# Neighbourhood attention with two heads' keys and queries in one tile, scores by 64 rows, a third set of bias tables

## The chip, the cores and the metric

The kernel runs on one core of one Trainium2 chip. The core has the matrix engine PE (weights are loaded into it by LDWEIGHTS, listed apart as PEld, and the other operand streams past), the vector engine DVE, the scalar engine ACT, the engine POOL, and a queue SP from which almost all DMAs of this kernel are issued. Each engine carries out its own list of instructions in order; engines wait for each other on semaphores. The metric is the device time of one execution in microseconds, as the median of several runs.

## What is computed

One layer of a hybrid backbone over 1024 latent and 256 context tokens of width 1024: an input projection, a gated delta rule scan in two directions over four heads (group A), 2-D neighbourhood attention over eight heads of 64 (group B), an output projection and a SwiGLU feed-forward. The change concerns group B. Cut to what matters:

```python
def neighborhood_attention(q, k, v, k_ctx, v_ctx, rpb, rows):
    ...
        q_r = lax.dynamic_index_in_dim(qg, r, axis=1, keepdims=False)
        k_r = lax.dynamic_slice_in_dim(kg, r0, win_rows, axis=1)[:, :, key_cols]
        v_r = lax.dynamic_slice_in_dim(vg, r0, win_rows, axis=1)[:, :, key_cols]
        ...
        s_win = jnp.einsum("bnqhd,binchd->bhnqic", q_r, k_r) + bias
        s_win = jnp.where(col_valid[:, :, None, :], s_win, -jnp.inf)
        s_ctx = jnp.einsum("bnqhd,bkhd->bhnqk", q_r, k_ctx)
        s = jnp.concatenate([s_win.reshape(B, H, N_COL_BLK, QB_W, n_win), s_ctx], axis=-1)
        p = jax.nn.softmax(s, axis=-1)
        o = (jnp.einsum("bhnqic,binchd->bnqhd", p_win, v_r)
             + jnp.einsum("bhnqk,bkhd->bnqhd", p[..., n_win:], v_ctx))
```

Each latent query has one softmax over its window (with a learned bias) and all 256 context keys.

## The kernel before

**Stages.** Up to about 540 us the kernel computes the projections (class `Block`, tiles blk, hh, hl, whi, wlo), and beside them the inverses of 32 x 32 blocks (N, WK, ut) and the preparation of the scan's chunks (`preps`: kk, fx, y, matmuls pr). Then the scan (`scan`, two directions, ten chunks each; its matmuls have ps as output) and neighbourhood attention (`attention`) run interleaved up to about 765 us. The output projection and the feed-forward follow.

**Attention by pairs of heads.** `attention` is a generator. It walks over 32 units: four pairs of heads, and for each 8 blocks of 128 queries (TILES). A unit is one call of `pair`, which has three parts, separated by yields: the scores of both heads and their softmax (tile sc in PSUM, then ex), the transposes of the probabilities (again sc, copied by ACT to pt), and the product with the values (vc for context, vw for the window), whose result goes to na. The first part of unit n+1 is issued before the second part of unit n. Scores, transposes and values share three PSUM slots of 1024 float32 each (`slot`).

**Scores.** Queries and keys have 64 dimensions and are kept as two float16 numbers, a high and a low part, whose sum is the float32 value. Before, the 128 rows of the array hold for one head the high part of the queries in the first 64 and the low part in the last 64 (qs), and the keys' high part stands twice, in both halves (kh), and so does the low part (kl). One matmul with kh and one with kl so give all four products of high and low. A head has 640 scores a query, 256 context and 384 window ones, in a PSUM slot that starts at column 0 for the first head and 128 for the second (AT, WIN, CTX), so that no matmul crosses a bank.

**Values.** The two heads of a unit write to two halves of the columns of the array (64 columns each), in turn.

**Softmax.** DVE adds the bias table and takes the maximum (L364), negates it (L365), ACT takes the exponential with its sum (L366), DVE inverts the sum (L367) and scales (L368). The bias tables bt (two, one for each head) exist in two sets; `biases` loads the next set by DMA (L325).

**What sets the order.** `beside` draws the attention forward by PACE = 0.72 steps for each step of a scan direction. The order on each engine is then made by a scheduler from the program's order and its estimate of when things are ready, so an edit at one place can move instructions elsewhere. Some matmuls are pinned in program order; those of attention are not.

**Storage.** The normed keys and queries are written to DRAM by `Block.norm` (L574, tile hl16, one DMA for each part and head) and loaded by `load` in `attention` (L306 to L309, five DMAs a head). A float32 matmul shows in the trace as two instructions, a float16 one or a transpose as one.

## Time and profile before

| | |
|---|---|
| runs | 1516.56, 1509.77, 1509.48 us; median 1509.77 |
| profiled execution | 1511.45 us, its span 1509.7 us |
| granted clock of PE, mean | 0.99 |
| HBM traffic | 201.01 MB read, 68.98 MB written |
| scores, kh and kl together | 320 matmuls, 74.3 us busy |
| transposes of ex | 320 matmuls, 45.9 us busy |
| values, vc and vw together | 640 instructions, 83.2 us busy |

A row of the timeline gives start, duration, engine, line, operation, output<-inputs, for a matmul rows*columns of the array that it uses, the shape and type of its operand, and how many instructions are merged (x8). PE is pipelined: a matmul's duration holds the way through the array, so several stand in the trace at once, and their pace is read from the starts. Busy time of PE therefore overstates how much it does. In brackets stands for how long the engine sat idle before, and what ended that.

### The profile page before, as it was taken

The page shows a single profiled execution, that of the slowest core. Times are in us where ns is not written, and L with a number is a line of the kernel's source. Part 1 is how long each engine was busy: PE and PEld are TensorE (multiplying, and loading weights), DVE is VectorE, ACT ScalarE, POOL GpSimd, SP SyncE. Part 2 cuts the span into 40 slices and gives each one's busy share as a digit, 9 for nine tenths or more (in the row PEclk, how much of TensorE's full clock was granted, in tenths as well). Part 3 has the DMA queues.
Part 4 walks back from the last instruction along what each step waited for, and adds up shares of the span by engine and source line. Part 5 has one row for each costly group of instructions (what it writes and reads, how often), then busy time and mean ns, then how long its engine had stood idle before and what let it go on. Part 6 is the DMA issues. An engine that isn't in the chain of part 4 may idle for free.

```text
span 1509.7 us, 23086 instructions
## 1 busy us (share of the span) xinstructions
PE 1453.5 (96%) x8365; PEld 1205.7 (80%) x8365; DVE 1007.9 (67%) x1908; ACT 704.7 (47%) x1379; POOL 164.6 (11%) x191
## 2 busy tenths in 40 slices
PE   6999998799999999999989999999999999999998
PEld 2789887678877778898777888788888888888887
DVE  4886579445587418789966499655555666698652
ACT  6443362585256536667732374333333334354441
POOL 0153500243134300000000000000000000000000
PEclk9999999999999999999999999999999999999999
DMA  9377133566378799986339216333333325798742
GB/s 366 119 237 234 35 107 121 180 180 194 98 235 249 214 272 289 264 225 184 116 119 313 99 35 208 106 105 105 105 105 105 104 94 173 267 365 281 237 153 84
DMA packets 198851, 267.35 MB, mean 177 GB/s; under 512 B 15232, under 2 KB 106960, under 8 KB 197712
## 3 DMA queue, kind: packets, MB, share of 16 engines
q1 hardware_dynamic: 198016, 265.49, 55.1%
q8 instruction: 66, 1.08, 0.3%
q10 hardware_dynamic: 720, 0.37, 0.1%
q14 instruction: 49, 0.40, 0.1%
HBM read 201.01 MB, written 68.98 MB: 179 GB/s over the span
## 4 chain that ended last, share of the span: by engine, by line
PE 67%; DVE 8%; DMA 5%; ACT 5%; issue 2%; SPq 1%; POOL 0%; ACTq 0%; DVEq 0%; POOLq 0%
PE ps L102 45%; PE blk L102 10%; PE sc L102 5%; PE pr L102 3%; DMA nv_d<-zt 2%; PE sc L106 2%; PE m L102 1%; DMA wad<-wa 1%; DMA wraw<-w_nqk 1%; DVE acc L256 1%; ACT ex L366 1%; DVE x L1616 1%; DVE cacc L520 1%; SPq L1093 1%; DVE ex L368 0%
## 5 line engine op out<-in xcount | busy, mean ns | idle before, releaser
L102 PE MATMUL ps<-hT,uhi 128*128 128x512 f32 x496 | 146.8, 390 | 0.9 <-DVE e L1737 0.8
L102 PE MATMUL ps<-lT,uhi 128*128 128x512 f32 x496 | 146.4, 389 | 0.0
L102 PE MATMUL ps<-hT,ulo 128*128 128x512 f32 x496 | 146.2, 389 | 0.0
L102 PE MATMUL blk<-hh,whi 128*128 128x512 f32 (+1 forms) x456 | 139.3, 397 | 2.1 <-ACT hh L748 1.8
L102 PE MATMUL blk<-hl,whi 128*128 128x512 f32 (+1 forms) x456 | 130.1, 379 | 0.0
L102 PE MATMUL blk<-hh,wlo 128*128 128x512 f32 (+1 forms) x456 | 129.9, 378 | 0.0
L102 PE MATMUL ps<-hB,uhi 128*128 128x512 f32 x436 | 129.1, 390 | 0.0
L102 PE MATMUL ps<-lB,uhi 128*128 128x512 f32 x436 | 128.9, 389 | 0.0
L102 PE MATMUL ps<-hB,ulo 128*128 128x512 f32 x436 | 128.7, 389 | 0.0
L1446 ACT CAST uhi<-ws 128x512 fp32r<-128x512 f32 x91 | 54.7, 623 | 145.4 <-PE ps L102 75.8
L1446 ACT CAST uhi<-wq 128x512 fp32r<-128x512 f32 x101 | 60.4, 621 | 130.8 <-PE ps L102 66.3
L1447 DVE TENSOR_TENSOR ulo<-wq,uhi 128x512 fp32r<-128x512 f32 x101 | 67.1, 686 | 65.6 <-ACT uhi L1446 36.1
L102 PEld LDWEIGHTS ps<-hT,uhi 128*128 128x128 f32 x496 | 92.9, 188 | 20.7 <-ACT uhi L1446 1.2
L102 PEld LDWEIGHTS ps<-lT,uhi 128*128 128x128 f32 x496 | 93.0, 188 | 19.7 <-DVE lT L1600 0.4
L102 PEld LDWEIGHTS ps<-hT,ulo 128*128 128x128 f32 x496 | 93.1, 188 | 19.4
L102 PEld LDWEIGHTS ps<-hB,uhi 128*128 128x128 f32 x436 | 81.8, 188 | 17.4 <-issue 0.5
L102 PEld LDWEIGHTS ps<-lB,uhi 128*128 128x128 f32 x436 | 81.8, 188 | 17.3 <-DVE lB L1600 0.4
L102 PEld LDWEIGHTS ps<-hB,ulo 128*128 128x128 f32 x436 | 81.8, 188 | 17.0
L102 PEld LDWEIGHTS blk<-hh,wlo 128*128 128x128 f32 x456 | 80.9, 191 | 17.9 <-issue 1.7
L102 PEld LDWEIGHTS blk<-hl,whi 128*128 128x128 f32 x456 | 81.6, 192 | 15.5
L102 PEld LDWEIGHTS blk<-hh,whi 128*128 128x128 f32 x456 | 77.3, 192 | 19.4 <-ACT hh L748 3.7
L1447 DVE TENSOR_TENSOR ulo<-ws,uhi 128x512 fp32r<-128x512 f32 x91 | 60.6, 685 | 36.2 <-ACT uhi L1446 28.1
(337 smaller groups left out, 3020.1 us busy)
## 6 DMA issues: line engine op xcount, KB each, us to landing
wq<-w_fo SPq DMA_DIRECT2D x99, 256.0 KB
wq<-w_gu SPq DMA_DIRECT2D x88, 256.0 KB
wad<-wa SPq DMA_DIRECT2D x64, 256.0 KB
t_d<-g SPq DMA_DIRECT2D x22, 512.0 KB
fr<-t_d SPq DMA_DIRECT2D x44, 256.0 KB
bt<-rpb SPq DMA_DIRECT2D x48, 192.0 KB
f_d<-g SPq DMA_DIRECT2D x33, 256.0 KB
fr<-f_d SPq DMA_DIRECT2D x33, 256.0 KB
```

Source lines behind the costliest of these rows:

```text
L102: i = nc.tensor.matmul(*args, **kw)
L106: i = nc.tensor.transpose(*args, **kw)
L256: dve.scalar_tensor_tensor(acc2, x, sc, acc2, op0=OP.mult, op1=OP.add)
L366: act.activation(ex, ex, AF.Exp, bias=m[:, 1:2], accum_out=m[:, 2:3])
L520: dve.scalar_tensor_tensor(acc[:, d0:d1], raw[:, d0 + o:d1 + o], cw[:, blk, tap:tap + 1], acc[:, d0:d1], op0=OP.mult, op1=OP.add)
L1093: sp.dma_start(vw_d[:, cb, ch], vlat[4 * ch:4 * ch + 4, BLKS[cb]:BLKS[cb] + 32])
L1446: act.copy(hi, self.raw[key])
L1447: dve.tensor_tensor(lo, self.raw[key], hi.bitcast(F32), OP.subtract)
L1616: dve.tensor_tensor(B[at][:, k], B[x][:, k], B.get(y, B["B11"])[:, k], OP.subtract)
```

## The change

Keys and queries of two heads share a tile: the 64 dimensions of the first head in the first 64 rows, of the second in the last 64; high and low parts lie behind one another. A unit's scores become 24 matmuls of 64 rows: three parts (256 context, 256 and 128 window scores), for each the four products of high and low, for each the two heads in turn on the two row halves, into two PSUM slots. Context comes first for both heads, so AT, WIN and CTX go, and the order of the values is the same for both. Keys and queries are stored by one DMA a block instead of four and loaded by two a pair of heads instead of ten. The room this frees holds a third set of bias tables, a fifth ex and a fourth pt.

```diff
-    nq_d = dram.tile([NAH, 2, ND, L], F16, name="nq_d", tag="nq_d")
-    nk_d = dram.tile([2, NAH, ND, T], F16, name="nk_d", tag="nk_d")
+    nq_d = dram.tile([NAH // 2, 128, 2, L], F16, name="nq_d", tag="nq_d")
+    nk_d = dram.tile([NAH // 2, 128, 2, T], F16, name="nk_d", tag="nk_d")
...
-        def load(hd):
-            qs = nw.tile([128, L], F16, name="qs", tag="qs", bufs=4)
-            kh = nw.tile([128, T], F16, name="kh", tag="kh", bufs=4)
-            kl = nw.tile([128, T], F16, name="kl", tag="kl", bufs=4)
-            sp.dma_start(qs, nq_d[hd].rearrange("i d t -> (i d) t"))
-            for i in range(2):
-                sp.dma_start(kh[i * 64:i * 64 + 64], nk_d[0, hd])
-                sp.dma_start(kl[i * 64:i * 64 + 64], nk_d[1, hd])
-            return qs, kh, kl
+        def queries(hp):
+            qs = nw.tile([128, 2, L], F16, name="qs", tag="qs", bufs=2)
+            sp.dma_start(qs, nq_d[hp])
+            return qs
+
+        def keys(hp):
+            kx = nw.tile([128, 2, T], F16, name="kx", tag="kx", bufs=2)
+            sp.dma_start(kx, nk_d[hp])
+            return kx
...
-                      for i in range(2)]
+                      for i in range(3)]
...
-                out = lasting_bt[tables[1] % 2]
+                out = lasting_bt[tables[1] % 3]
...
-            for u, (head, w0, bt) in enumerate(zip(heads, WIN, bts)):
-                qs, kh, kl = head
-                sc = slot()[:, AT[u]:AT[u] + 640]
-                q = qs[:, (half * 4 + cb) * 128:(half * 4 + cb + 1) * 128]
...
-                for n0, n1, ks in parts:
-                    for i in range(2):
-                        pe.matmul(sc[:, n0:n1], q, ks[i], start=i == 0, stop=i == 1)
+            qs, kx = heads
+            scs = [slot()[:, :640] for _ in range(2)]
+            q = [[qs[u * ND:u * ND + ND, i, (half * 4 + cb) * 128:(half * 4 + cb + 1) * 128] for i in range(2)]
+                 for u in range(2)]
+            kw = [[kx[u * ND:u * ND + ND, i, CT:].rearrange("p (r c) -> p r c", c=64)[
+                :, r0:r0 + 12, BLKS[cb]:BLKS[cb] + 32] for i in range(2)] for u in range(2)]
+            for n0, n1, part in ((0, CT, None), (CT, 512, slice(0, 8)), (512, 640, slice(8, 12))):
+                for j in range(4):
+                    for u in range(2):
+                        k = kw[u][j % 2][:, part] if part else kx[u * ND:u * ND + ND, j % 2, 0:CT]
+                        pe.matmul(scs[u][:, n0:n1], q[u][j // 2], k, start=j == 0, stop=j == 3)
+            for u, (sc, bt) in enumerate(zip(scs, bts)):
                 m = mx[:, u]
-                ex = nw.tile([128, 640], F32, name="ex", tag="ex", bufs=4)
+                ex = nw.tile([128, 640], F32, name="ex", tag="ex", bufs=5)
...
-                pt = nw.tile([128, 640], F32, name="pt", tag="pt", bufs=3)
+                pt = nw.tile([128, 640], F32, name="pt", tag="pt", bufs=4)
...
-                for i, x in enumerate((h16, l16)):
-                    for hb in range(2):
-                        hd = 2 * self.i + hb
-                        dst = nk_d[i, hd] if isk else nq_d[hd, i]
-                        sp.dma_start(dst, x[hb * 64:hb * 64 + 64, t0:])
+                sp.dma_start((nk_d if isk else nq_d)[i], hl16[:, :, t0:])
```

The scheduler makes a new order from this, in two places that matter below.

The first is on PE late in the attention, between the scores of one unit (sc<-kh,qs and sc<-kl,qs), the values of the unit before (sc<-pt,vc and sc<-pt,vw) and the transposes that follow (sc<-cst,ex). Before:

```order
L102 LDWEIGHTS qs
L102 MATMUL sc<-kh,qs 128x384
L102 LDWEIGHTS qs
L102 MATMUL sc<-kl,qs 128x384
L102 MATMUL sc<-pt,vc 64x128
L102 MATMUL sc<-pt,vw 64x128
L102 MATMUL sc<-pt,vc 64x128
L102 MATMUL sc<-pt,vw 64x128 x4
L102 MATMUL sc<-pt,vc 64x128
L102 MATMUL sc<-pt,vw 64x128
L102 MATMUL sc<-pt,vc 64x128
L106 MATMUL sc<-cst,ex 128x128 x10
```

And now, with the tiles' numbers (sc_6953 is the first head's slot, sc_6954 the second's, sc_6882 the slot of the unit before):

```order
L99 MATMUL sc_6953<-kx_6389,qs_6184 128x256
L99 LDWEIGHTS qs_6184
L99 MATMUL sc_6954<-kx_6389,qs_6184 128x256
L99 LDWEIGHTS qs_6184
L99 MATMUL sc_6954<-kx_6389,qs_6184 128x256
L99 LDWEIGHTS qs_6184
L99 MATMUL sc_6953<-kx_6389,qs_6184 128x256
L99 LDWEIGHTS qs_6184
L99 MATMUL sc_6954<-kx_6389,qs_6184 128x256
L99 LDWEIGHTS qs_6184
L99 MATMUL sc_6953<-kx_6389,qs_6184 128x256
L99 MATMUL sc_6882<-pt_6880,vc_6186 64x128
```

The values now cut into a unit's scores after 7 of 24, and the other 17 follow them; before, a unit's ten scores stood whole ahead of them here.

The second place is on DVE in the projection stage, where the block inverses end (ut and WK are their transposed and scaled forms, which go to DRAM as x_d for the scan's preparation) beside the norm of the last block of keys (cacc, hl). Before:

```order
L967 STREAM_TRANSPOSE ut<-WK 128x1280
L970 TENSOR_TENSOR ut<-ut,NB 128x1280
L556 SCALAR_TENSOR_TENSOR cacc<-cacc,qkw,cr 128x1280
L967 STREAM_TRANSPOSE ut<-WK 128x1280
L562 TENSOR_TENSOR hl_2523<-cacc,hl_2523 128x1280
L970 TENSOR_TENSOR WK<-WK,NB 128x1280
L556 SCALAR_TENSOR_TENSOR cacc<-cacc,qkw,cr 128x1024
```

Now:

```order
L958 STREAM_TRANSPOSE ut<-WK 128x1280
L961 TENSOR_TENSOR ut<-ut,NB 128x1280
L958 STREAM_TRANSPOSE ut<-WK 128x1280
L551 SCALAR_TENSOR_TENSOR cacc<-cacc,qkw,cr 128x1280
L961 TENSOR_TENSOR WK<-WK,NB 128x1280
L557 TENSOR_TENSOR hl_2514<-cacc,hl_2514 128x1280
L1007 TENSOR_TENSOR kk<-kk,e 128x512 x2
```

The second transpose moved ahead of cacc, and hl behind the scaling of WK. On PE, the first matmul of the preparation (pr<-fx,kk) stands 16 matmuls of the projection earlier than before.

More of the change, by code (lines that the diff above doesn't have):

```diff
@@ L53 @@
 NCONST = 4 * 128 + 4 * 32
-WIN = (256, 0)
-AT = (0, 128)
 TILES = ((0, 0), (0, 1), (1, 1), (2, 1), (2, 0), (1, 0), (3, 0), (3, 1))
-CTX = {256: slice(0, 256), 0: slice(384, 640)}
 PACE = 0.72
@@ L322, in biases @@
             if tables[0] != key:
-                out = lasting_bt[tables[1] % 2]
-                for u, w0 in enumerate(WIN):
-                    sp.dma_start(out[u][:, w0:w0 + 384], a["rpb"][2 * hp + u, half, CASE[cb]])
+                out = lasting_bt[tables[1] % 3]
+                for u in range(2):
+                    sp.dma_start(out[u][:, CT:], a["rpb"][2 * hp + u, half, CASE[cb]])
                 tables[:] = key, tables[1] + 1
-            return lasting_bt[(tables[1] - 1) % 2]
+            return lasting_bt[(tables[1] - 1) % 3]
         def values(hp, half, cb):
@@ L380, in pair @@
             yield 1
-            o = held[:, AT[1] + 640:AT[1] + 768]
+            o = held[:, 640:768]
+            vals = [vc[:, i] for i in range(2)] + [vw[:, i] for i in range(3)]
             for j in range(5):
-                for u, (w0, pt) in enumerate(zip(WIN, pts)):
-                    vals = [vc[:, i] for i in range(2)] + [vw[:, i] for i in range(3)]
-                    vv = (vals[j] if w0 else vals[(j + 2) % 5])[:, u * ND:u * ND + ND]
+                for u, pt in enumerate(pts):
+                    vv = vals[j][:, u * ND:u * ND + ND]
                     pe.matmul(o[u * ND:u * ND + ND], vv, pt[:, j * 128:(j + 1) * 128], start=j == 0, stop=j == 4)
@@ L394, in attention @@
         order = [(hp, half, cb) for hp in range(NAH // 2) for cb, half in TILES]
-        heads = {0: [load(0), load(1)]}
+        heads = {0: [queries(0), keys(0)]}
         vcs = {0: context(0)}
@@ L402, in attention @@
             if at in (4, 6) and hp + 1 < NAH // 2:
-                heads.setdefault(hp + 1, []).append(load(2 * hp + at // 2))
+                heads.setdefault(hp + 1, []).append((queries if at == 4 else keys)(hp + 1))
                 if at == 4:
```

14 lines of the change are left out of this document (4 added, 10 removed).

## The prediction

> **What bounds the kernel now.** I read the page first, then the busy time of the stretches in which neighbourhood attention runs, then what PE waits for there, and last single instructions. The page's engine line says PE; the scores run only between 555 and 765 us, so two stretches of that time matter.
>
> ```profile
> PE 1453.5 (96%) x8365; PEld 1205.7 (80%) x8365; DVE 1007.9 (67%) x1908; ACT 704.7 (47%) x1379; POOL 164.6 (11%) x191
> ```
>
> ```profile
> core 0: us, PE busy (x) PEld busy (x) DVE busy (x) ACT busy (x) POOL busy (x), PEclk, DMA share, GB/s
> 555.00:672.00 117.00, 113.98 (x1106) 101.75 (x1103) 92.58 (x306) 79.35 (x214) 0.00 (x0) 1.00 0.96 262
> 672.00:765.00 93.00, 88.00 (x860) 75.36 (x858) 86.96 (x345) 65.26 (x179) 2.57 (x2) 1.00 0.50 150
> ```
>
> ```profile
> 671.06 1.06 PE L102 MATMUL ps<-vn,y 128*128 128x128 f32 x8
> ```
>
> The row of PE's timeline marks the boundary: the vn,y matmuls of the seventh scan step. Up to there PE is busy 97% and DVE 79%: PE alone is the limit, and what is added to PE is added to the time. Behind it the output gates of the scan are on DVE as well: DVE is busy 93.5%, PE 94.6%. There PE has 5 us in which it stands still, and added work hides in part behind DVE. DMA is full in the first stretch (0.96), so the question is whether anybody waits for a landing. The waits of PE, of its weight loads (PEld) and of the SP queue answer it:
>
> ```profile
> PE sc L102 <- ACT pt L378: 2.0, 4, 1.0
> PE sc L106 <- DVE ex L368: 2.0, 1, 2.0
> PE sc L106 <- DVE mx L364: 1.1, 3, 0.5
> PEld sc L102 <- ACT pt L378: 7.3, 18, 1.4
> SPq L325 <- DVE mx L364: 22.2, 13, 7.4
> ```
>
> PE's longest totals are 2.0 us, all for ACT or DVE and none for a DMA. SP's queue does stand 22.2 us behind a bias table that is still in use (L325), which is what the third set takes away; but no engine's list of waits shows a landed table, key or query being late. So I cost the fewer loads (40 issues of keys and queries before, 8 now) and the third table at nothing: the prefetch already covers them. If that cover were gone, the price would be at most those 22.2 us of queue, in a stretch with DMA half idle.
>
> **The scores themselves.** A pair of heads has 10 score matmuls of 128 rows before, 2 x 2 x 640 columns, and 24 of 64 rows now, 2 x 4 x 640 columns. What a column costs, and what it costs PE to change the shape in which its array is used, stands in one place of the trace, where the value matmuls (128*64: two halves of the columns, vc and vw are tiles of values) come between whole-array matmuls:
>
> ```profile
> 594.37 1.06 PE L102 MATMUL ps<-vn,at 128*128 128x128 f32 x8
> 595.36 0.32 PE L102 MATMUL sc<-pt,vc 128*64 128x128 f32 x1
> 595.36 0.32 PE L102 MATMUL sc<-pt,vw 128*64 128x128 f32 x1
> 595.52 0.27 PE L102 MATMUL sc<-pt,vc 128*64 128x128 f32 x1
> 595.52 0.27 PE L102 MATMUL sc<-pt,vw 128*64 128x128 f32 x1
> 595.62 0.27 PE L102 MATMUL sc<-pt,vc 128*64 128x128 f32 x1
> 595.63 0.27 PE L102 MATMUL sc<-pt,vw 128*64 128x128 f32 x1
> ...
> 596.18 0.27 PE L102 MATMUL sc<-pt,vc 128*64 128x128 f32 x1
> 596.38 1.16 PE L102 MATMUL ps<-vk,kt 128*128 128x128 f32 x8
> 597.47 0.32 PE L102 MATMUL sc<-pt,vw 128*64 128x128 f32 x1
> ...
> 597.63 0.27 PE L102 MATMUL sc<-pt,vc 128*64 128x128 f32 x1
> 597.84 0.28 PE L102 MATMUL sc<-kh,qs 128*128 128x256 f16 x1
> 597.96 0.27 PE L102 MATMUL sc<-kl,qs 128*128 128x256 f16 x1
> 598.07 0.33 PE L102 MATMUL sc<-kh,qs 128*128 128x384 f16 x1
> ```
>
> ```profile
> 695.35 0.22 PE L102 MATMUL sc<-kh,qs 128*128 128x128 f16 x1
> 695.40 0.22 PE L102 MATMUL sc<-kl,qs 128*128 128x128 f16 x1
> 695.46 0.27 PE L102 MATMUL sc<-kh,qs 128*128 128x256 f16 x1
> ```
>
> Read the starts, not the durations (0.27 us is the pipeline). A score of 256 columns takes 0.11 us to the next (597.96 to 598.07), one of 128 takes 0.055 (695.35 to 695.46, two of them): 2560 columns a pair of heads are 1.10 us, 35.2 us for 32. Two value matmuls on the two column halves start together and the next two 0.105 us later, as long as one alone: halves of the columns do run side by side. The trace has no matmul on half of the rows. I take it that the row halves do the same, so 24 scores cost 12 slots, again 1.10 us; the other end is one after the other, 2.20 us. I am nearer to the first, since the column halves are the nearest row.
>
> The Trainium skill speaks against a full gain: its page "TensorE: Matmul & The Clock Gate", Part 3, gives a measured 3.07 for four row tiles side by side instead of 4. An estimate from that page would be 35.2 x 4 / 3.07 = 45.9 us of scores, 10.7 more, and by the shares used below 1529 us; the column halves of this trace lose nothing.
>
> **Changes of shape.** The eight vn,at start every (1.06 - 0.27) / 7 = 0.113 us, so the first value pair was due at 595.27 and started at 595.36, 0.09 late; its successor came 0.16 instead of 0.105 later. Into halves: 0.14 us. Back: the eight vk,kt were due at 596.29 and started at 596.38; they gave way at 597.47 instead of 597.28, of which 0.09 is the next change: 0.19 us out to float32. Out to a score: due 597.74, started 597.84, next after 0.12: 0.11 us. Leaving halves for the whole array costs 0.14 to 0.19; I use 0.165. Row halves are not in the trace; I take the same prices, with nothing as the lower end and twice this as the upper.
>
> Counted over PE's order from the first score to the last value matmul, the shape changes 79 times before (40 in, 39 out) and 155 times now: 60 times into row halves, 33 into column halves, 62 to the whole array. Before: 40 x 0.14 + 16 x 0.11 (to a score) + 23 x 0.165 = 11.2 us. Now: 60 x 0.11 + 33 x 0.14 + 62 x 0.165 = 21.5 us. That is 10.3 us more on PE: 41 of the added changes lie before the boundary (5.5 us), 35 behind it (4.8 us).
>
> **Halves left alone.** In the order the two heads do not always alternate (in the piece shown above, sc_6954 stands twice in a row, and the values cut in when one head is a score ahead). With each half as a queue of its own and the column prices above, the 768 scores in their order take 38.6 us instead of 35.2: 1.3 us more before the boundary, 2.1 behind it.
>
> **The third PSUM slot.** Both heads' scores now end together, where the first head's were done 0.55 us sooner. The second head's transposes of the pair before take the slot that the first head's maximum frees:
>
> ```profile
> L364 DVE CUSTOM_DVE_ANT_0 ex<-sc,bt 128x640 f32<-128x640 f32 x64 | 51.6, 816 | 32.1 <-issue 31.0 <-PE sc L102 0.9
> ```
>
> That is 0.82 us plus some 0.1 of hand-over after the last score; PE has five transposes (0.55) and mostly four scan matmuls (0.45) between, which just covers it; where nothing lies between (three places) 0.35 us is lost. While PE waits, the scan's matmuls queue behind. I charge 1.0 us (ends: 0, and 32 x 0.35 = 11).
>
> **The larger pools** (ex 5, pt 4) would shorten PEld's 7.3 us for pt. But ACT copies pt late because it waits for transposes, not for a free pt. I charge 0, lower end -4 us.
>
> **The projection.** Stores of keys and queries fall from 32 issues to 8, and the scheduler orders DVE and PE anew around the block inverses:
>
> ```profile
> 265.35 0.53 PE L106 MATMUL m<-cst,N 80*128 80x80 f32 x2 [5.45 <-DVE N L952]
> ...
> 275.29 1.49 DVE L970 TENSOR_TENSOR ut<-ut,NB 128x1280 f32<-128x1280 f32 x1
> ...
> 285.40 1.55 DVE L556 SCALAR_TENSOR_TENSOR cacc<-cacc,qkw,cr 128x1280 f32<-128x1280 f32 x1 [8.62 <-ACT cr L553]
> 286.87 1.50 DVE L967 STREAM_TRANSPOSE ut<-WK 128x1280 f32<-128x1280 f32 x1
> 288.30 1.47 DVE L562 TENSOR_TENSOR hl<-cacc,hl 128x1280 f16<-128x1280 f32 x1
> 289.69 3.69 DVE L970 TENSOR_TENSOR WK<-WK,NB 128x1280 f32<-128x1280 f32 x1
> 293.40 0.32 SPq L972 DMA_DIRECT2D x_d<-WK  x1
> 302.25 2.02 PE L102 MATMUL pr<-fx,kk 128*128 128x96 f32 x8 [6.98 <-DVE kk L1016]
> ```
>
> PE stood 7 us for the first preparation of a scan chunk, whose chain hangs on the x_d store at 293.40. Now the transpose goes ahead of cacc and hl behind WK*NB, so that store is 2.9 us sooner (5.0 if WK*NB takes 1.5 us like its sister, no longer beside POOL's wlo). But PE reaches the matmul 16 matmuls earlier (3.6 us of blk work at 0.226), and the wait at 265.35 moves 7 matmuls forward (1.5 us). PE then resumes at 297.3 to 299.4 with 3.6 us still to do: 1.4 us gained to 0.7 lost. I take -0.3, and 2 us either way for the rest of this stage.
>
> **The sum.** Up to the boundary in full: 5.5 + 1.3 = 6.8 us. Behind it 4.8 + 2.1 = 6.9, of which I charge half, 3.4, since DVE is as full as PE (ends 0 and 6.9). With 1.0 and -0.3 it is +10.9 us. The profiled execution took 1511.45 us, so it would be 1522.3; the runs shown have their median at 1509.77, 1.7 lower, so I predict **1521 us**.
>
> **Rivals.** (1) Row halves run one after the other. For: no such row in the trace. Against: the column halves. Every pair of heads pays 1.10 us more: 18 pairs before the boundary 19.8, 14 behind it 15.4, of which three quarters show, since the cover is spent; the lone halves (1.3 and half of 2.1) fall away: +39.9, 1550 us.
>
> (2) Weight loads bind. Each score loads its own queries:
>
> ```profile
> L102 PEld LDWEIGHTS <-qs 128*128 128x128 f16 x320 | 28.2, 98 | 5.7 <-issue 3.1
> ```
>
> One load lasts 98 ns and the densest rows show one per 0.055 us (695.35 to 695.40). The eight 128-column scores of a pair now want two loads in 0.055 us. If loads of the two halves take turns, they need 0.44 us instead of 0.22: 18 x 0.22 = 4.0 and half of 3.1, 5.5 on top: +16.4, 1526 us. [...]
>
> (3) Not slower: a change into or out of row halves is free, because the next queries go into rows that the last matmul does not use or has left. It decides whether the first score starts on time behind another shape. Then of the 155 changes 20 x 0.14 + 14 x 0.165 = 5.1 us remain, 6.1 less than before: 3.3 less before the boundary, half of 2.8 behind it; with the lone halves, +1.3 and half of 2.1, and 0.7 it is -1.6 us, 1508 us, and with pt's -4, 1504. Against it: each change of this trace costs, in either direction. The Trainium skill, "TensorEngine Tiling (Array Packing)", Key Properties, says that a change of the tiling mode drains the array; by that rule rival 3 falls away, and the trace agrees for column halves (0.09 us).
>
> (4) The change does not do what it says, so that SP's 22.2 us stay: it costs nothing by the lists of waits, and lies within the forecast.
>
> **Chances.** Forecast 0.61 (own range 1514 to 1527), rival 1 0.08, rival 2 0.13, rival 3 0.18. A measurement of this kernel tells about 0.5%, 7.5 us, from no change: 1502 and 1517 are the bounds. Slower: 0.46 of the forecast, and rivals 1 and 2, 0.67. Within: 0.15 of the forecast and 0.11 of rival 3, 0.26. Faster: the rest of rival 3, 0.07. The range 1506 to 1534 leaves out rival 1, some of rival 3 and the ends of single costs.
>
> **What would show it.** Pairs of 64*128 scores that start within 0.01 us, 0.11 us to the next pair (0.22: rival 1; 0.11 for 128 columns: rival 2); the first score of a group 0.1 us late (on time: rival 3); the stretch up to the boundary some 7 us longer, that behind it 3; PE's waits for pt and for a landing about as now. If the second stretch gets shorter, the larger pools are worth more than I give them; if the time before 555 us moves by over 2 us, the new order there is what I misjudged.

## The result and the profile after

| | before | after |
|---|---|---|
| median of four runs, us | 1512.49 (1509.48 to 1516.56) | 1535.61 (1532.89 to 1536.74) |
| ratio, 95% interval | | 1.015, 1.013 to 1.017 |
| profiled execution, its span, us | 1511.45, 1509.7 | 1536.74, 1534.7 |

The change made the kernel 1.5% slower, some 23 us where 11 were forecast. The engine line of the page after, to be read against the one shown before:

```profile
PE 1470.2 (96%) x8813; PEld 1213.8 (79%) x8813; DVE 1013.5 (66%) x1908; ACT 708.1 (46%) x1379; POOL 160.2 (10%) x193
```

PE is busy for 16.7 us more and stands still for 8 more, in a span 25.0 us longer. (In the table of the time before, 74.3 and 83.2 us each add up two groups that overlap in time. Taken together, the scores keep PE busy for 43.9 us and the values for 44.8; after the change the scores take 50.7.) To see where, I cut both traces at the same events instead of the same times: at the first score, and at the first matmul of vn,y in the second, the seventh and the tenth step of the scan (the first step has none). The seventh is the boundary of the prediction. Rows of PE's timeline, the kernel before, then after:

```profile
554.78 0.27 PE L102 MATMUL sc<-kh,qs 128*128 128x256 f16 x1
567.41 0.39 PE L102 MATMUL ps<-vn,y 128*128 128x128 f32 x2
667.75 0.50 PE L102 MATMUL ps<-vn,y 128*128 128x128 f32 x3
761.62 0.61 PE L102 MATMUL ps<-vn,y 128*128 128x128 f32 x4
```

```profile
552.24 2.14 PE L99 MATMUL sc<-kx,qs 64*128 64x256 f16 x32
571.69 0.50 PE L99 MATMUL ps<-vn,y 128*128 128x128 f32 x3
677.21 0.61 PE L99 MATMUL ps<-vn,y 128*128 128x128 f32 x4
784.87 0.83 PE L99 MATMUL ps<-vn,y 128*128 128x128 f32 x6
```

The stretches between them in the table by windows (columns: window, length, then busy time of PE, PEld, DVE, ACT, POOL, the granted clock, DMA share, GB/s), before, then after:

```profile
554.80:567.40 12.60, 10.61 (x99) 9.11 (x97) 8.74 (x29) 9.58 (x28) 0.00 (x0) 1.00 0.99 298
567.40:667.70 100.30, 99.26 (x973) 88.64 (x972) 79.66 (x263) 66.61 (x177) 0.00 (x0) 1.00 0.95 255
667.70:761.60 93.90, 88.90 (x868) 76.45 (x868) 89.04 (x353) 67.87 (x187) 2.57 (x2) 1.00 0.54 162
```

```profile
552.20:571.70 19.50, 16.98 (x146) 13.85 (x146) 8.86 (x31) 10.85 (x30) 0.00 (x0) 0.74 0.95 297
571.70:677.20 105.50, 102.87 (x1154) 89.29 (x1153) 78.81 (x256) 66.77 (x176) 0.00 (x0) 1.00 0.63 192
677.20:784.90 107.70, 96.35 (x1082) 80.21 (x1081) 95.58 (x354) 69.11 (x188) 2.55 (x2) 0.98 0.46 135
```

Three losses: 6.9 us in the first step, 5.2 in the stretch up to the boundary, 13.8 behind it. What lies ahead of the first score came 2.5 us sooner; what lies behind the last of these rows takes 1.7 us longer.

The same marks do not hold quite the same work. Counted in the traces, the stretch up to the boundary has the scores of 15 units before and of 14 after, and 145 and 140 transposes; behind it they are 14 and 15 units, 160 and 155 transposes. An estimate from the pace of the rows (0.11 us for 256 float16 columns or for one float32 instruction of 128, a pair of halves counted once) is 90.9 and 79.9 us of PE work before, 89.2 and 79.5 after. For equal work the losses are thus nearer 6.9 us up to the boundary and 14.2 behind it.

DMA has become much emptier, 0.95 to 0.63, and nothing got faster by it. In the last stretch PE now stands still for 11.4 us instead of 5.0, and DVE's busy share fell from 95% to 89%: the added work is not hidden by DVE there. What PE waits for in that stretch, before and after (total us, times, longest):

```profile
PE sc L102 <- ACT pt L378: 1.6, 3, 1.0
PE sc L106 <- DVE mx L364: 1.1, 3, 0.5
PE sc L106 <- DVE na L391: 0.7, 2, 0.4
PE sc L106 <- DVE orr L1279: 0.5, 1, 0.5
```

```profile
PE sc L103 <- DVE mx L359: 5.0, 9, 1.4
PE sc L99 <- ACT pt L373: 3.8, 8, 1.2
PE sc L103 <- DVE na L386: 0.9, 3, 0.4
PE sc L103 <- ACT pt L373: 0.8, 1, 0.8
```

Transposes (L106, now L103) wait for the slot that a maximum frees, 1.1 us before and 5.0 after, values (L102, now L99) for the copy to pt, 1.6 and 3.8; the four lines of each list together are 3.9 and 10.5. Changes of shape in that stretch, counted in the traces, went from 34 to 74; by the prediction's prices that is 4.8 and 10.2 us. With the prediction's 2.1 us of lone halves, an estimate that no run measured by itself, the three make 6.6 + 5.4 + 2.1 = 14.1, about what was lost.

### The profile page after: what moved, and what is told of

The parts are those of the page before. It is cut to its first block, busy times and chain, and to the rows that moved or that the text cites. A ratio compares the mean times of both kernels' runs of the same rounds, so it can differ in the third digit from the quotient of the medians.

```text
span 1534.7 us, 23940 instructions
## 1 busy us (share of the span) xinstructions
PE 1470.2 (96%) x8813; PEld 1213.8 (79%) x8813; DVE 1013.5 (66%) x1908; ACT 708.1 (46%) x1379; POOL 160.2 (10%) x193
## 4 chain that ended last, share of the span: by engine, by line
PE 70%; DVE 15%; ACT 6%; DMA 4%; issue 3%; POOL 1%; SPq 0%; ACTq 0%; DVEq 0%; POOLq 0%
PE ps L99 43%; PE blk L99 15%; PE sc L99 4%; PE pr L99 3%; PE m L99 3%; PE sc L103 2%; DVE tt L938 2%; ACT ex L361 2%; DMA wad<-wa 2%; DVE N L940 2%; DVE cacc L495 1%; DVE acc L253 1%; ACT pt L373 1%; PE m L103 1%; DVE cacc L515 1%
## 5 line engine op out<-in xcount | busy, mean ns | idle before, releaser
L99 PE MATMUL ps<-hT,uhi 128*128 128x512 f32 x496 | 146.7, 390 | 1.1 <-DVE e L1728 1.0
L99 PE MATMUL ps<-lT,uhi 128*128 128x512 f32 x496 | 146.4, 389 | 0.0
L99 PE MATMUL ps<-hT,ulo 128*128 128x512 f32 x496 | 146.3, 389 | 0.0
L99 PE MATMUL blk<-hh,whi 128*128 128x512 f32 (+1 forms) x456 | 139.3, 397 | 2.0 <-ACT hh L739 1.3
L99 PE MATMUL blk<-hh,wlo 128*128 128x512 f32 (+1 forms) x456 | 129.5, 378 | 0.0
L99 PE MATMUL ps<-hB,uhi 128*128 128x512 f32 x436 | 129.1, 390 | 0.0
L99 PE MATMUL ps<-lB,uhi 128*128 128x512 f32 x436 | 128.8, 389 | 0.0
L99 PE MATMUL ps<-hB,ulo 128*128 128x512 f32 x436 | 128.8, 389 | 0.0
L99 PE MATMUL blk<-hl,whi 128*128 128x512 f32 (+1 forms) x456 | 128.6, 375 | 0.0
L99 PEld LDWEIGHTS ps<-hT,uhi 128*128 128x128 f32 x496 | 93.0, 188 | 20.9 <-ACT uhi L1437 1.4
L99 PEld LDWEIGHTS ps<-lT,uhi 128*128 128x128 f32 x496 | 93.0, 188 | 19.7 <-DVE lT L1591 0.4
L99 PEld LDWEIGHTS ps<-hT,ulo 128*128 128x128 f32 x496 | 93.1, 188 | 19.5
L99 PEld LDWEIGHTS ps<-hB,uhi 128*128 128x128 f32 x436 | 81.8, 188 | 17.4 <-issue 0.5
L99 PEld LDWEIGHTS ps<-lB,uhi 128*128 128x128 f32 x436 | 81.8, 188 | 17.3 <-DVE lB L1591 0.4
L99 PEld LDWEIGHTS ps<-hB,ulo 128*128 128x128 f32 x436 | 81.8, 188 | 17.1
L99 PEld LDWEIGHTS blk<-hh,wlo 128*128 128x128 f32 x456 | 80.5, 190 | 17.4 <-issue 2.5
L99 PEld LDWEIGHTS blk<-hl,whi 128*128 128x128 f32 x456 | 80.6, 189 | 15.5
L99 PEld LDWEIGHTS blk<-hh,whi 128*128 128x128 f32 x456 | 77.4, 192 | 19.4 <-ACT hh L739 3.0
```

Source lines behind the costliest of these rows:

```text
L99: i = nc.tensor.matmul(*args, **kw)
```

## The experiments

The theory after the result: the row halves' work on PE shows in full, since nothing covers it; on top come new waits for a slot and for pt, and a first step that is delayed by DMA. All times in the table are cut from each kernel's trace as above: the first score's time, the first step from there, the stretch up to the boundary, the one behind it, in us.

| kernel | median | ratio, 95% | first score | first step | up to boundary | behind it |
|---|---|---|---|---|---|---|
| before | | | 554.8 | 12.6 | 100.3 | 93.9 |
| after | 1535.61 | 1.015 (1.013 to 1.017) | 552.2 | 19.5 | 105.5 | 107.7 |
| b_storage | 1516.35 | 1.0029 (1.0014 to 1.0043) | 554.9 | 16.4 | 102.0 | 93.9 |
| b_joint | 1521.42 | 1.0058 (1.0033 to 1.0083) | 551.1 | 12.6 | 102.2 | 96.9 |
| b_load | 1516.88 | 1.0031 (1.0019 to 1.0044) | 552.8 | 13.0 | 104.1 | 96.5 |
| b_load2 | 1523.21 | 1.0068 (1.0044 to 1.0092) | 552.3 | 13.6 | 105.7 | 98.9 |
| b_shape | 1515.50 | 1.0014 (0.9995 to 1.0033) | 552.1 | 12.8 | 102.0 | 96.5 |
| b_vk | 1511.38 | 0.9989 (0.9977 to 1.0002) | 552.3 | 11.1 | 100.4 | 93.9 |
| a_pools | 1533.94 | 1.0149 (1.0128 to 1.0171) | 553.5 | 16.5 | 105.4 | 107.1 |
| a_whole | 1517.97 | 1.0038 (1.0020 to 1.0056) | 553.3 | 15.4 | 101.6 | 96.5 |
| a_vk | 1534.74 | 1.0135 (1.0102 to 1.0169) | 550.4 | 14.5 | 105.5 | 107.0 |
| a_high | 1537.26 | 1.0161 (1.0126 to 1.0196) | 552.9 | 20.1 | 109.6 | 105.3 |
| b_two | 1521.62 | 1.0061 (1.0045 to 1.0078) | 554.2 | 15.2 | 103.5 | 97.7 |

b_ stands for an edit of the kernel before, a_ for one of the changed kernel. The first score came anywhere from 551 to 555 us in those kernels that change nothing ahead of it (b_joint, b_load, b_load2, b_shape, b_two, b_vk; up to 545 us their order on PE, DVE and ACT is that of the kernel before): the 2.5 us by which the changed kernel was sooner are within what two executions differ, and cannot be called an effect of the edit. The stretches of single executions repeat better: b_vk has those of before within 0.1 us, a_pools and a_vk those of after within 0.7.

As above, the marks cut off different amounts of work in some kernels. PE's work between them, estimated in the same way, in us:

| kernel | up to boundary | behind it |
|---|---|---|
| before | 90.9 | 79.9 |
| after, a_pools, a_vk | 89.2 | 79.5 |
| b_joint | 90.7 | 78.2 |
| b_load | 95.4 | 88.1 |
| b_load2 | 95.9 | 85.7 |
| a_whole | 90.7 | 78.3 |
| a_high | 89.2 | 78.3 |

### The row halves: scores back on the whole array (a_whole)

```diff
-                for j in range(4):
+                for j in range(2):
                     for u in range(2):
-                        k = kw[u][j % 2][:, part] if part else kx[u * ND:u * ND + ND, j % 2, 0:CT]
-                        pe.matmul(scs[u][:, n0:n1], q[u][j // 2], k, start=j == 0, stop=j == 3)
+                        k = kw[j][:, part] if part else kx[:, j, 0:CT]
+                        pe.matmul(scs[u][:, n0:n1], q[j], k, start=j == 0, stop=j == 1)
```

> The changed kernel with its scores on the whole array: 12 matmuls of 128 rows a unit in place of 24 of 64, still both heads in turn and ending together, with the new storage, the third set of tables and the larger pools (a score so holds the sum over both heads' dimensions and two of the four products of high and low, not the score of the reference). Some 75 changes of shape remain of 155, and no half is left alone. Theory: what the row halves cost goes, what the joint end and the new order in front of the scan cost stays: the stretch from the first to the seventh step's vn,y falls from 105.5 us to about 102 (as in the kernels with the storage alone or the joint end alone), the stretch behind it from 107.7 to 97, in all 13 to 15 us below the changed kernel, 1.005 of the kernel before. Rival: the loss behind the boundary comes from the third set, the pools or the fewer and larger loads, and both stretches stay within 2 us of the changed kernel's.

Measured: 3.9 and 11.2 us less than the changed kernel in the two stretches (for equal work 5.4 and 10.0), 4.1 in the first step, 17.6 us of median, more than the 13 to 15 expected. The theory's numbers for the stretches (102 and 97) were met by 101.6 and 96.5. So the row halves, with the order that the scheduler makes for them, and not the tables, pools or loads, which this kernel shares, are the bulk of the loss. Behind the boundary its busy times and PE's waits are these; the waits sum to 7.8, against 10.5 with row halves:

```profile
670.30:766.80 96.50, 87.86 (x888) 76.43 (x888) 90.08 (x352) 68.07 (x186) 2.54 (x2) 1.00 0.50 149
```

```profile
PE sc L103 <- DVE nwt L197: 2.6, 3, 0.9
PE sc L103 <- ACT pt L372: 2.3, 3, 0.8
PE sc L103 <- DVE mx L359: 1.8, 3, 0.6
PE ps L99 <- DVE vn L1213: 0.6, 1, 0.6
PE sc L99 <- ACT pt L372: 0.5, 3, 0.2
```

Of the 11.2 us there, 2.7 are longer waits, 5.9 changes of shape (74 against 32) and 2.1 lone halves by the prediction's prices, and about 1.2 are work that stands on the other side of a mark. That makes 11.9, so the estimates are some 0.7 us too large.

### The price of a change of shape alone (b_shape)

```diff
+                if u:
+                    pe.matmul(whole[:, 896:1024], qs[0:64, 0:128], kh[0:64, 0:128], start=True, stop=True)
```

> The kernel before with one added score matmul of 64 rows and 128 columns (float16) a unit, which nothing reads, in front of the second head's scores; 27 of the 32 stand between scores of 128 rows. It adds 0.055 us of columns and two changes of shape a unit. Theory: a change costs 0.11 us wherever it stands between busy matmuls, so a unit costs 0.275 us more, 8.8 us in all, some 4 in the stretch from the first to the seventh step's vn,y and some 4 behind it, of which four fifths show as they did behind the values: 7 us, 1.004 to 1.006 of the kernel before. Rival: a change costs far more than its delay (it empties PE's queue of weight loads, say), 0.2 us or more, 14 us and above. Second rival: under 0.05 us, and the loss of the changed kernel is waits alone: below 4 us.

PE's timeline around one such matmul (whole is the second head's slot; the row that says x2 merges the added 64-row matmul with the next score of the head):

```profile
580.67 0.22 PE L102 MATMUL sc<-kl,qs 128*128 128x128 f16 x1
580.82 0.44 PE L102 MATMUL sc<-kh,qs 64*128 64x128 f16 x2
581.10 0.27 PE L102 MATMUL sc<-kl,qs 128*128 128x256 f16 x1
```

From 580.67 to 581.10 are 0.43 us; the columns of the three matmuls between take 0.055 + 0.055 + 0.11 = 0.22. Two changes cost 0.21 us. Over the 27 places where it stands between two whole-array scores the first start came 0.097 us late at the median on the way in and 0.104 on the way out: the prediction's 0.11 holds, 0.14 and 0.165 too (0.095 late for column halves, and the second pair 0.05 to 0.10). In the two stretches 1.7 and 2.6 us of the 8 showed, and the ratio cannot be told from 1. Theory right on the price, too high on how much shows: by the median the whole time grew by less than the second rival's 4 us, but not because a change costs under 0.05. The Trainium skill, "TensorEngine Tiling (Array Packing)", Key Properties, says that a change of the tiling mode drains the array; this trace agrees, with 0.1 us for it.

### Is added work covered? (b_load, b_load2)

```diff
                 held = slot()
+                pe.matmul(held[:, 896:1024], ident, ident, start=True, stop=True)
```

> The kernel before with a float32 matmul of 128x128 that nothing reads in front of each set of transposes: two a unit, 64 in all, 0.226 us each, without a change of shape (77 instead of 79): 8.1 us of PE work before the boundary, 6.3 behind it. Theory: PE is the limit in both stretches, and all of it shows: +8.1 and +6.3, 1526 us for the 1511.5 of the profile. Rival, the prediction's step: behind the boundary DVE is as full as PE and half is covered: +8.1 and +3.2, 1523. Second rival: it is covered wholly there: +8.1, 1520. The step of 555 to 570 us should show PEclk 1.00 as before if the dip of the changed kernel is due to its scores.

```diff
+            for _ in range(2):
+                pe.matmul(held[:, 896:1024], pt[:, 0:128], ident, start=True, stop=True)
...
```

> The kernel before with the same 64 added matmuls (0.226 us each, 14.5 us, 8.1 of it before the boundary and 6.3 behind it), but two behind each unit's values in place of one in front of each set of transposes. In front of the transposes, where PE often has to wait for the scaled ex, 4.2 and 2.6 us of them showed. Theory: what is covered depends on the place: behind the values PE does not wait, so nearly all shows, 7 to 8 and 5 to 6 us, 1.008 to 1.009 of the kernel before. Rival, the prediction's step generalised: PE shares the limit with DVE in both stretches and half is covered wherever the work stands: 4 and 3 us.

Counted in the traces, the stretches hold 28 and 32 of the added matmuls in b_load (6.3 and 7.2 us), 30 and 30 in b_load2 (6.8 and 6.8). The two stretches grew by 3.8 and 2.6 us in b_load, by 5.4 and 5.0 in b_load2. But the scores of one unit stand behind the boundary in both instead of ahead of it. For equal work, by the table above, 5.6 of 6.3 and 1.6 of 7.2 us showed in front of the transposes, 7.2 of 6.8 and 6.0 of 6.8 behind the values. So up to the boundary nearly all of it shows at either place: PE is the limit there, as the prediction had it. Behind the boundary the place decides. The busy times of that stretch, b_load and then b_load2:

```profile
669.90:766.40 96.50, 95.37 (x943) 84.57 (x942) 89.99 (x355) 67.92 (x187) 2.55 (x2) 1.00 0.54 159
671.60:770.50 98.90, 93.78 (x928) 83.34 (x926) 90.65 (x353) 67.10 (x184) 2.54 (x2) 1.00 0.54 157
```

PE stood still for 5.0 us there in the kernel before, for 1.1 in b_load and for 5.1 in b_load2: work in front of the transposes fills what PE would wait, work behind the values leaves it. What PE and its weight loads waited for in b_load:

```profile
PEld sc L102 <- ACT pt L379: 4.7, 13, 0.6
...
PE sc L102 <- ACT pt L379: 0.7, 3, 0.3
```

The last line is all of PE's own waiting that is listed for that stretch of b_load, where the four lines of the kernel before make 3.9. My first theory (all of it shows) held up to the boundary and failed behind it for b_load; that of b_load2 (nearly all shows) is borne out. Neither place shows the prediction's half: less than that in front of the transposes, most of it behind the values. And for the changed kernel any such rate was wrong, since its waits grew.

### Both heads' scores ending together (b_joint)

```diff
+            for k in range(6):
+                for js in jobs:
+                    if k < len(js):
+                        o, q, x, i = js[k]
+                        pe.matmul(o, q, x, start=i == 0, stop=i == 1)
```

> The kernel before, with the scores of the two heads in turn: the same 10 matmuls of 128 rows a unit, no new shapes (75 changes of shape instead of 79), but both heads' scores now end together, as in the changed kernel. Theory: the joint end delays the maxima and with them the slot for the next transposes; PE's and PEld's waits for mx rise from 3.2 us to 8 or more, and the stretch behind the vn,y matmuls of the seventh step grows by 3 to 6 us from its 93.2. Rival, the prediction's figure: 1.0 us in all, 0.5 behind the boundary. Second rival: nothing, and the waits for mx of the changed kernel come from its 64-row scores, which in its order are cut into more pieces.

1.9 us up to the boundary and 3.0 behind it, at the lower end of the theory, five times the prediction's 1.0 together; for equal work it is 2.1 and 4.7. The profiled execution is the fastest of five, and by the ratio the whole kernel lost 8.8 us, so these are rather too small. PE stood still for 9.0 us behind the boundary instead of 5.0:

```profile
665.80:762.80 97.00, 88.03 (x860) 75.02 (x860) 89.95 (x352) 68.01 (x186) 2.55 (x2) 1.00 0.53 158
```

PE's waits for mx rose only to 1.8; others grew with them (nwt 2.6, pt 3.0). The later maxima thus seem to delay DVE's and ACT's other work as well. These waits are those of a_whole, line for line within 0.2 us, and so is the length of the stretch: what a_whole keeps of the loss behind the boundary is most likely the joint end.

### Storage alone, and the wait in the first step (b_storage, a_vk, b_vk)

```diff
+                sp.dma_start((nk_d if isk else nq_d)[i], hl16[:, :, t0:])
...
+            at = slice(hd % 2 * 64, hd % 2 * 64 + 64)
             for i in range(2):
+                sp.dma_start(qs[i * 64:i * 64 + 64], nq_d[hd // 2, at, i])
+                sp.dma_start(kh[i * 64:i * 64 + 64], nk_d[hd // 2, at, 0])
+                sp.dma_start(kl[i * 64:i * 64 + 64], nk_d[hd // 2, at, 1])
```

> The kernel before with the new storage alone: keys and queries are stored by one DMA a block; attention is as before, with its 640 scores a head on 128 rows, and reads the same values (6 loads a head instead of 5). Theory: the 2.5 us by which the first score came sooner (554.78 to 552.24) are due to this edit alone, through the order of DVE and PE around the block inverses; the time is 2.5 us below the kernel before, 0.998 of it, all of it ahead of the first score, and the ten scan steps last as before within 0.5 us each. Rival, the prediction's own figure: -0.3 us; then the 2.5 us came from something else, such as the memsets and loads of attention.

Both numbers failed: it is slower by 0.3%, by 3.8 us in the first step and 1.7 in the stretch up to the boundary. ACT's rows of the first step's vk in the kernel before, b_storage and the changed kernel, one below the other:

```profile
555.97 2.18 ACT L1244 ACTIVATE vk<-ps,KB 128x128 f32<-128x128 f32 x8 [3.12 <-DMA zT_d<-zt]
```

```profile
558.26 2.17 ACT L1241 ACTIVATE vk<-ps,KB 128x128 f32<-128x128 f32 x8 [5.26 <-DMA zT_d<-zt]
```

```profile
554.80 2.18 ACT L1235 ACTIVATE vk<-ps,KB 128x128 f32<-128x128 f32 x8 [4.59 <-DMA zT_d<-zt]
```

vk takes the memory of the last zt, so ACT has to wait until that tile's store has landed. ACT waits 1.5 to 2.1 us longer here than in the kernel before, and its exponentials of the first unit stand behind those rows. Why the store lands later is not shown. The wait is 4.3 to 5.5 us in all six kernels with the new storage that have it, and 3.1 in six of the seven with the old one; but in the seventh, b_two, it is 4.9, with the same issues of SP around the store as before. So the loads around it are not the whole reason. A second part of b_storage's 3.8 us goes with a granted clock of 0.50 that lasted about 3.4 us in that step (see the last section). The 1.7 us are a table that landed late: in the third step DVE waits for bt.

```profile
600.06 0.82 DVE L365 CUSTOM_DVE_ANT_0 ex<-sc,bt 128x640 f32<-128x640 f32 x1 [2.16 <-DMA bt<-rpb]
```

To take that wait away, the first step's rows go to vn, which is idle there:

```diff
-            vk = work("vk")
+            vk = work("vk") if s is not None else vn
```

> The changed kernel in which the first scan step of each direction writes its scaled rows to tile vn, which is idle there, instead of vk. The result is the same; vk lies where the last zt lay, so that ACT had to wait until that tile's store had landed, vn does not, and the order of PE is unchanged. Theory: the first step is longer because that store lands 4.6 us after its issue instead of 3.1 (the loads of keys, queries and tables share the DMA engines with it), and the half clock follows from the pause of PE; without the wait the step from the first score to the first vn,y falls from 16.6 to 19.5 us to 13 to 14, and the time by 3 to 5 us. Rival: the exponentials of the first unit set it, and it stays over 16 us.

> The kernel before with the first scan step's rows in vn instead of vk, so that ACT does not wait 3.1 us for the store of the last zt. Order on PE unchanged. Theory: the step from the first score to the first vn,y (12.6 us) gets 1 to 2 us shorter, since the exponentials of the first unit stand behind those rows on ACT: 0.9985 to 1.000 of the kernel before. Rival: PE waits there for the exponentials whose start is set by DVE's maxima, and nothing changes.

```profile
549.66 2.17 ACT L1235 ACTIVATE vn<-ps,KB 128x128 f32<-128x128 f32 x8 [1.30 <-issue]
```

This is the row of a_vk. The wait is gone (1.30 us instead of 4.59) and the first step takes 14.5 us instead of 16.5 (a_pools) or 19.5, a little more than the theory's 13 to 14; in b_vk it takes 11.1 instead of 12.6, as expected. In the whole time neither can be told from its parent, so the 3 to 5 us expected of a_vk did not show: its median is 0.9 us lower, and the profiled execution, 1529.3 us, is the fastest of its four by 5 us.

### The old sizes (a_pools)

```diff
-                      for i in range(3)]
+                      for i in range(2)]
...
-                ex = nw.tile([128, 640], F32, name="ex", tag="ex", bufs=5)
+                ex = nw.tile([128, 640], F32, name="ex", tag="ex", bufs=4)
...
-                pt = nw.tile([128, 640], F32, name="pt", tag="pt", bufs=4)
+                pt = nw.tile([128, 640], F32, name="pt", tag="pt", bufs=3)
```

> The changed kernel with the old sizes: two sets of bias tables, four ex, three pt. Its order on PE is the same as that of the changed kernel. Theory: larger pools and the third set are worth nothing that can be measured, since no engine waits for a landed table and ACT's copies to pt wait for transposes; within 2 us of the changed kernel's 1535.6 (1.015 of the kernel before), SP's wait for the maxima back at 20 us or so. Rival: they hide part of the loss, and without them it is up to 4 us slower still. In the first scan step the half clock of 557 to 567 us is there again if it belongs to the order of the scores, and is not if it was chance.

The third set, the fifth ex and the fourth pt are worth nothing that can be measured, 1.0149 against 1.015. SP's queue stands 19.1 us for the maxima with two sets and 18.0 with three: the third set takes 1.1 us of that wait away, and not the 22.2 of the prediction. The half clock of the first step was not there, with the same order on PE.

### Scores drawn together (a_high)

```diff
+            with tc.high_priority():
```

> The changed kernel with its scores at high priority for the scheduler: of 60 groups of scores 35 remain, each whole (24, or 12 on a half each), so that no half is left alone; changes of shape 148 instead of 155, but more of them at the column halves. By the prices of the prediction the lone halves fall away (3.4 us) and the shape changes cost the same 21.5 us. Theory: 3 to 5 us less than the changed kernel, most of it behind the boundary. Rival: scores drawn forward hold two of three slots for longer, the transposes wait for a slot, and it is no faster.

It is no faster, as the rival says. Behind the boundary 2.4 us were gained, but one unit's scores stand ahead of the first step's end instead, so that it is 1.2 for equal work, and the changes of shape there fell from 74 to 59; a gain from the lone halves cannot be read from it. Up to the boundary 4.1 us were lost, and not by the rival's waits for a slot: PE is busy there for 109.4 of 109.6 us. What took them is open. PE's wait for mx behind the boundary stayed at 5.5 us though each group of scores is whole, so the pieces of the order were not what made it.

### Other slots (a_four, b_four, b_four_vk, b_two)

In the first three, one tile of 3072 columns is cut into four slots of 768; in the fourth there are two slots of 1536, one for both heads' scores and one for both heads' transposes.

```diff
-            return psum[-1].tile([128, 1024], F32, name="sc", tag="sc", bufs=3)
+            return next(sct)
...
+        while True:
+            for k in (0, 2, 1, 3):
+                yield big[:, k * 768:k * 768 + 768]
```

> The changed kernel with four PSUM slots of 768 columns in place of three of 1024 (in the order 0, 2, 1, 3, so that a unit's scores never share a bank). The scores hold two slots and the transposes find two others. On PE, 31 of 32 units are now whole, 117 changes of shape instead of 155, no lone halves: by the prices 32 x 0.11 + 32 x 0.14 + 53 x 0.165 = 16.7 us of changes instead of 21.5, and 3.4 us of lone halves less. Theory: the waits of PE for mx and na behind the boundary (5.9 us) go, the stretch behind it falls from 107.5 us by 9 to 11, and the one up to it from 105.5 by 2 to 3: 1521 to 1525 us, 1.007 to 1.010 of the kernel before. Rival: the slot was not what PE waited for but DVE itself, the mx waits move to ex, and only the 8 us of shape work go, half of them visible.

> The kernel before, scores on 128 rows and head by head, its old storage and two sets of tables, with the same four slots of 768 columns; context comes first for both heads. 63 changes of shape instead of 79 (2.4 us by the prices), every unit's values whole. Theory: what PE waits for mx, na and ACT's pt behind the boundary (3.4 us) goes in part, and the rests of the scan's own waits stay: 3 to 6 us below the kernel before, 0.996 to 0.998. Rival: the order by which whole units stand together puts waits for ex and pt in place of it, and it is the same within 1 us.

> The same with the first scan step's rows in vn instead of vk, so that ACT does not wait for the store of the last zt. In the changed kernel that took the first step from 16.5 or 19.5 to 14.5 us. Theory: ACT starts those rows up to 3 us sooner and the exponentials of the first unit with them: 1 to 3 us below the kernel with four slots alone, 0.994 to 0.997 of the kernel before. Rival: in the order of the kernel before that wait hides beside the first scores, and nothing is gained.

These failed by far: 1635.62, 1610.88 and 1614.80 us, 1.0800 (1.0778 to 1.0821), 1.0647 (1.0632 to 1.0663) and 1.0672 (1.0656 to 1.0688). The units came one behind the other. Rows of b_four, of PE, ACT and DVE:

```profile
800.66 1.33 PE L106 MATMUL sc<-cst,ex 128*128 128x128 f32 x5 [0.84 <-ACT pt L380]
802.08 0.69 ACT L380 COPY pt<-sc 128x640 f32<-128x640 f32 x1 [1.48 <-PE sc L106]
802.82 1.12 PE L102 MATMUL sc<-pt,vc 128*64 128x128 f32 x8 [0.84 <-ACT pt L380]
...
805.91 0.37 PE L102 MATMUL sc<-kh,qs 128*128 128x256 f16 x1 [0.69 <-DVE na L393]
```

The second head's transposes wait for the copy of the first, the next unit's scores for the na of the last; 117 us of attention were left behind the first vn,y of the tenth step (752 to 869 us). Whether the banks made it so, of which the expectation of b_two speaks, or that the four slots are pieces of one tile, was not tested. These runs tell nothing on the three slots.

```diff
-            return psum[-1].tile([128, 1024], F32, name="sc", tag="sc", bufs=3)
+            return psum[-1].tile([128, 1536], F32, name="sc", tag="sc", bufs=2)
```

> The kernel before with two PSUM slots of 1536 columns in place of three of 1024: both heads' scores in one, both heads' transposes and values in the other, no bank shared between the two (with the four slots of 768 neighbours shared a bank, and the units ran one behind the other). Scores on 128 rows, old storage; 79 changes of shape as before. PE's transposes no longer wait for a maximum. Theory of the slot: the waits for mx (1.1 us on PE behind the boundary before, 5.0 in the changed kernel) are gone, 1 to 3 us below the kernel before, 0.998 to 0.999 of it. Rival: both copies of ACT to pt now come behind all ten transposes and the transposes wait for the values of the unit before, so the waits for pt and na grow by more than that and it is 2 to 6 us slower.

The rival again, and by more than its 2 to 6 us: the wait of transposes for the slot's maximum is gone, but PE's for pt grew from 1.6 to 7.4 us (from 667 us on; that for na did not grow), and the kernel is 0.6% or 9 us slower. Scores now wait for mx instead:

```profile
PE sc L102 <- ACT pt L381: 7.4, 9, 1.7
PE sc L102 <- DVE mx L367: 2.0, 3, 0.7
```

No version was found that beats the kernel before by more than its measurement can tell.

## Why the prediction was right and wrong

**Right: what a score and a change of shape cost.** In the changed kernel a whole unit stands in the trace as one row, and the next row shows the slot's wait:

```profile
580.49 1.27 PE L99 MATMUL sc<-kx,qs 64*128 64x256 f16 x24
582.15 0.77 PE L103 MATMUL sc<-cst,ex 128*128 128x128 f32 x5 [0.39 <-DVE na L386]
```

24 scores, 16 of 256 columns and 8 of 128, would take 16 x 0.11 + 8 x 0.055 = 2.2 us in a row; with the pipeline's 0.2 they took 1.27. The halves run side by side without loss, so rivals 1 (one after the other) and 2 (weight loads bind) fall. The 3.07 of 4 that the Trainium skill gives ("TensorE: Matmul & The Clock Gate", Part 3) is for four row tiles; these two halves show no such loss. Rival 3 (a change costs nothing) falls with the 0.097 us of b_shape, and in the changed kernel the first score behind a float32 matmul of the whole array starts 0.207 us after it at the median, where the next such matmul would after 0.112. Rival 4 is largely what happened, and cost nothing: SP stands 18.0 us for the tables instead of 22.2.

**Right: the larger pools and the third table at 0** (a_pools).

**Nearly right: the stretch up to the boundary.** 5.2 us came up to the first vn,y of the seventh step, 6.9 for equal work, where 6.8 were charged over a stretch that held the first step too. The reason given, "PE alone is the limit, and what is added to PE is added to the time", held for the added work of b_load and b_load2. That the number fits as well is in part luck: for equal work the row halves cost 5.4 of it (a_whole), and most of the rest is the joint end, which the 6.8 did not contain.

**Wrong: the stretch behind the boundary.** The step that failed is "added work hides in part behind DVE" and with it "behind it 4.8 + 2.1 = 6.9, of which I charge half, 3.4, since DVE is as full as PE". Two busy shares of 94% do not say which engine covers which. What covers added work is a wait of PE at that very place (b_load left 1.1 of 5.0 us of standstill, b_load2 all of it), and this change made such waits longer instead of filling them: 11.4 us. The row halves cost 11.2 us there (a_whole; 10.0 for equal work), three times the charge, though the 6.9 was about right: the changes counted in the traces come to 5.4 us by its prices where 4.8 were charged, and of the 2.1 for lone halves there is no measurement.

**Wrong: the third slot at 1.0 us.** The term was mis-sized: ending both heads' scores together costs 1.9 + 3.0 us by itself (b_joint), or more. I had worked out the cover of one kind of wait, the transposes' for the slot, and not that DVE and ACT get both heads' work at once; that this is the way in which it costs so much is inferred from the list of waits (nwt, pt), and no run separates it.

**Wrong: storage and loads at nothing.** That "no engine's list of waits shows a landed table, key or query being late" held for the lists of before. But the order of the issues changed, and what was late next were a store that frees vk's memory, by 1.5 to 2.1 us, and, in b_storage, a table, by 1.7. The trace had shown the first, 3.12 us of ACT for zT_d, and I did not ask what would happen if that landing moved. In the changed kernel the first step, for which nothing was charged, is 6.9 us longer; a_vk bounds the part of this wait at 2 us, the half clock took some 3 (19.5 against 16.5 in a_pools), 0.6 are five transposes that now stand in it, and the rest was not separated. Part of it may be scatter: the clock of a_pools, with the same order, did not fall, and b_two, with the old storage, has a late store and a first step of 15.2 us too.

**Not an effect: the projection.** -0.3 was charged with 2 us either way; the 2.5 us seen are within the scatter of that stage.

In sum: the change cost 15.1 us in the two stretches by its row halves, about 4 more, most likely by the joint end (a_whole stands 1.3 and 2.6 us above before), and 6.9 in the first step, of which some 3 are the half clock of that one execution.

## What to carry to other kernels

A matmul that uses half the array next to one that uses the whole pays about 0.1 us at each change, so small tiles gain only where they stand together; here they cost as many column slots as before and gained nothing to set against 76 changes. Whether added work shows is read at the place where it goes: ask whether the engine waits there now, and whether the edit makes that wait shorter or longer; the busy share of another engine does not answer it. When two traces are cut at the same events, count the work between them before comparing the times. When DMAs change, look also at stores whose tile's memory somebody needs next.

## What the hardware showed that was not expected

The first step of the changed kernel ran in large part at half the clock. Windows of its trace, columns as above:

```profile
555.00:560.00 5.00, 4.00 (x20) 3.24 (x21) 0.68 (x5) 4.97 (x14) 0.00 (x0) 0.70 1.08 357
560.00:565.00 5.00, 4.24 (x25) 3.46 (x24) 2.76 (x10) 2.87 (x13) 0.00 (x0) 0.50 1.10 347
565.00:570.00 5.00, 4.86 (x55) 3.77 (x55) 2.77 (x9) 1.86 (x5) 0.00 (x0) 0.78 1.03 307
```

By windows of one us the clock fell to 0.50 at 557 us and stayed there to 567, though PE was busy (4.24 us of 5 in the middle row). PE had stood still shortly before, for 1.6 us. In a_pools, with the same order, it stood for 2.2 us, the clock stayed at 1.00, and the step took 16.5 us instead of 19.5. The pause in the changed kernel, then that in a_pools:

```profile
556.00 1.23 PE L99 MATMUL ps<-vk,kt 128*128 128x128 f32 x8 [1.61 <-ACT vk L1235]
```

```profile
PE ps L99 <- ACT vk L1235: 2.2, 1, 2.2
```

b_storage, a_whole, b_two and a_four had shorter dips in that step, of about 3.4 us each at 0.50; in the kernel before PE paused for 2.0 us in it and the clock stayed at 1.00. All five kernels with a dip are among the seven in which ACT waits 4.3 us or more for the store of zt; of the seven, a_pools and a_high had none, and of the nine other kernels none had one. So the dip goes with the late store, though not always. The Trainium skill, "TensorE: Matmul & The Clock Gate", Part 1, has the clock halve after an idle window of some 3.4 us and come back after a busy one. Here the clock fell after a pause of half that length, did not fall after a longer one, and came back after 10 us though PE was busy; what decides it these runs do not show.
